# Starting branch A's output projection one or three units earlier in branch B's attention loop

## The chip, the cores and the metric

The kernel runs on one core of a Trainium2 chip. The metric is the device time of one execution in microseconds (us); smaller is better. Engine names are those of the profile: PE (matmul), PEld (weight load), DVE, ACT, POOL, and SP, which here only issues DMAs.

## The reference

One encoder layer, float32, applied to two inputs with the same weights: a prompt of 1024 tokens and a sample of 512 tokens, width 1024.

```python
xn = RMSNorm(x)
z  = xn @ W_in            # q_A k_A v_A q_B k_B v_B gate_A gate_B
o_A = grouped-query attention, q/k normalised per head, rotary positions
o_B = neighbourhood attention on the 64-wide token grid, 8 heads of 64, bias per head
mix = (sigmoid(gate_A) * (o_A @ W_pA) + sigmoid(gate_B) * (o_B @ W_pB)) @ W_out
x = x + mix
x = x + relu(RMSNorm(x) @ W_up)^2 @ W_down
y = RMSNorm(x)
```

The change touches the place where `o_A @ W_pA` is prepared while branch B's attention still runs.

## The kernel before, in words

The two inputs are two passes ("trunks") through the same code, one after the other. The sample goes first: it is the **short** trunk (T = 512, one block of 512 tokens, `first` is true, `JN == 2`). The prompt is the **long** trunk (T = 1024, two blocks, `JN == 1`).

Every matmul is done three times to keep float32 precision: a helper (`split`, lines 189 to 198) cuts a raw float32 tile into a high part, a copy on ACT (line 192), and a low part, two subtractions on DVE (line 198). `mm3` (lines 203 to 205) multiplies high by high, high by low and low by high.

A weight or a row block passes through three steps. SP issues a DMA into a raw tile, ACT and DVE split it into a slot, and PE uses the slot. The raw tiles come from one pool, `rawp`, with **three** buffers, and each tile holds its buffer from the issue of its DMA until DVE has read it for the low part. Weights (`load_cols`, DMA at line 228) and the rows of a branch's attention result (`load_o`, DMA at line 856) share these three buffers.

Branch B's attention runs in units, one head and one group of query blocks at a time: 16 units in the short trunk (two groups for each of 8 heads) and 32 in the long one (four). For each unit, `s_unit` makes the scores (`sbs` on PE, line 1007; maximum and exponent on DVE and ACT, lines 1009 and 1013, result `pbs`), `t_unit` of the unit before transposes them (`ptbs` on PE, split into `bhs` at lines 1041 and 1042), and `v_unit` of the unit before that multiplies by the values (`obs` on PE, line 1064). The values of a head come as 16 small DMAs (`vss`, line 914).

Between these steps PE is fed with **filler**: a generator that yields a few matmuls at a time. In the loop, the filler is first the gate of branch A and B (`gpss`, read out by ACT into `sgs` at line 463, stored by a DMA on ACT's queue as `zgs`), and from unit n-4 (short) or n-8 (long) on it is branch A's projection (`ppas`, with rows `oXs` and weights `w_pas`; the result goes to `mAs` at line 891). Every fourth (short) or eighth (long) unit the next head pair's queries and keys are made (`pqbs`, `pkbs` on PE; `qBs`, `kBs` on ACT and DVE, lines 949 to 969) from weights `w_bqs` and `w_bks`.

`proj_a` is a generator. Its first step, run by `next(pa)`, loads and splits its first weights (`raw_pas_0`, `w_pas_0`) and loads the four row blocks (`rawos_0_0` to `rawos_0_3`, 128 x 512 in the short trunk, 128 x 1024 in the long one) and splits the first three. The split of the fourth is put in the list `held`, which the loop empties one entry per unit. The line that calls `next(pa)` is the one changed.

Engines run their instructions strictly in the order of their streams. That order isn't the order of the code alone: a list scheduler takes the ready operation with the best priority, which is program order, and it hands out pool buffers at the moment it places an operation. So an operation that the code emits earlier can overtake others on every engine, and a buffer goes to whoever is placed first.

Of the kernel before, what the change touches and what calls it, by code (L numbers as in the profile page):

```python
# [61 lines left out]
def encoder(ctx: ExitStack, tc: tile.TileContext, xs, outs, w):  # L62
# [367 lines left out]
    def run(tr, nxt, first):  # L430
# [439 lines left out]
        def proj_a(pool, hold):  # L870
            nxt_w = load_cols(w["w_proj_a"][0], 0, P, f"pa{N}_0", slot_left)
            oA = load_o(0, hold)
            yield
            for c in range(NC8):
                wp = nxt_w
                if c + 1 < NC8:
                    nxt_w = load_cols(w["w_proj_a"][0], (c + 1) * P, P, f"pa{N}_{c + 1}", slot_left)
                else:
                    wp_b.append(load_cols(w["w_proj_b"][0], 0, P, f"pb{N}_0"))
                for tb in range(NB):  # L880
                    if c % 4 == 0:
                        mA[tb, c // 4] = slot([P, 4, 512], F32, f"mA{N}_{tb}_{c}", True)
                    p_ = mm(f"ppa{N}_{c}_{tb}")
                    cs = slice(tb * 512, tb * 512 + 512)
                    za = pool.tile([P, 512], F32, tag="za", name=f"za{N}_{c}_{tb}", bufs=2)
                    nc.sync.dma_start(za, zg[0][c * P : (c + 1) * P, cs])
                    for k in range(4):
                        mm3(p_, wp[k][0], wp[k][1], oA[k][:, 0, cs], oA[k][:, 1, cs], k == 0, k == 3)
                        if k < 3:
                            yield  # L890
                    nc.vector.scalar_tensor_tensor(
                        mA[tb, c // 4][:, c % 4, :], za, 1.0, p_, op0=ALU.add, op1=ALU.mult
                    )
                    yield
# [6 lines left out]
        with phase(f"phB{N}") as ph:  # L901
# [4 lines left out]
            def prep(h):  # L906
                rc = ph.tile([P, 16, 48], F32, tag="rect", name=f"rect{N}_{h}", bufs=2)
                nc.sync.dma_start(rc, biases[:, :, h].rearrange("r c i j -> (r c) i j"))
                rects[h] = rc
                v = slot([P, 4, rows // 4, P], F32R, f"vs{N}_{h}")  # L910
                for j in range(4):
                    c0 = (0, 8, 24, 32)[j]
                    for a in range(4):
                        nc.sync.dma_start(
                            v[a * 32 : a * 32 + 32, j, :, :].bitcast(F32),
                            vd[:, h, :].rearrange("(k a c) d -> a c k d", a=4, c=GRID_W)[a, c0 : c0 + 32],
                        )
                strips[h] = v

            def load_qk(pr, hold=None):  # L920
                return (
                    load_cols(win, 768 + pr * P, P, f"bq{N}_{pr}", hold=hold),
                    load_cols(win, 1280 + pr * P, P, f"bk{N}_{pr}", hold=hold),
                )
# [95 lines left out]
            def t_unit(u):  # L1020
                h, js = u
                nm = f"{N}_{h}_{js[0]}"
                p = PT[u]
                if halves == 2:
                    hl = ph.tile([P, 4, 2, 2, P], F32R, tag="bh", name=f"bh{nm}", bufs=2)
                    todo = [(hf, mm(f"ptb{nm}_{hf}")[:, : nkc * P], slice(hf, hf + nkc), hf) for hf in range(2)]
                else:
                    hl = ph.tile([P, 4, 2, 1, P], F32R, tag="bh", name=f"bh{nm}", bufs=2)
                    pt = mm(f"ptb{nm}")
                    todo = [(0, pt, slice(0, 4), 0)]  # L1030
                    for x in range(4):
                        nc.tensor.transpose(
                            pt[:, x * P : (x + 1) * P], p[:, x // 2, x % 2 * P : (x % 2 + 1) * P], ident
                        )
                for x, pt, ks, hf in todo:
                    if halves == 2:
                        for i in range(nkc):
                            nc.tensor.transpose(pt[:, i * P : (i + 1) * P], p[:, x, i * P : (i + 1) * P], ident)
                    src = pt.rearrange("p (k q) -> p k q", q=P)
                    dh, dl = hl[:, ks, 0, hf, :], hl[:, ks, 1, hf, :]  # L1040
                    nc.scalar.activation(dh, src, AF.Copy)
                    nc.vector.tensor_tensor(dl, src, dh.bitcast(F32), op=ALU.subtract)
                PT[u] = hl
# [63 lines left out]
            n = len(units)  # L1107
# [4 lines left out]
            for i in range(n + LS + LV):  # L1112
                if NB == 1:
                    f = 9 if i < 1 else 5 if i < n - 4 else 6 if i < n else 4 if i == n else 2
                else:
                    f = 0 if i == n - 10 else 5 + (i % 3 > 0) if i < n - 8 else 7
                if i < n:
                    s_unit(units[i])
                    if units[i][1][0] == 1 and units[i][0] + 1 < 8:
                        prep(units[i][0] + 1)  # L1120
                    if i % per == (6 if JN == 1 else 2) and i + 2 < n:
                        while held:
                            held.pop(0)()
                        qp = qkproj(i // per + 1, wqk, qk)
                        for _ in range(NC8):
                            next(qp)
                    if i % per == per - 1 and qp is not None:
                        for _ in qp:
                            pass
                        qp = None  # L1130
                fill.pull(f // 2)
                if 0 <= i - LS < n:
                    t_unit(units[i - LS])
                if held:
                    held.pop(0)()
                if i % per == 0 and i // per < 3:
                    wqk = load_qk(i // per + 1, held)
                if i == n - (6 if first else 9):
                    pa = proj_a(ph, held)
                    next(pa)  # L1140
                if i == n - (4 if JN == 2 else 8):
                    fill.drain()
                    fill.add(pa)
                if qp is not None and NB == 2:
                    for _ in range(NC8):
                        next(qp)
                fill.pull(f - f // 2)
                if 0 <= i - LS - LV < n:
                    v_unit(units[i - LS - LV])
# [730 lines left out]
    for i, tr in enumerate(trunks):  # L1880
        run(tr, trunks[i + 1] if i + 1 < len(trunks) else None, i == 0)
# [66 lines left out]
```

## Time and profile before

| | us |
|---|---|
| time, median of 3 runs | 2131.84 (2130.74 to 2132.03) |
| profiled execution, its own time | 2131.02 |
| its span, first to last instruction | 2129.2 |
| PE busy | 2111.4 (99%) |
| DVE busy | 1471.0 (69%) |
| ACT busy | 1117.3 (52%) |
| POOL busy | 390.7 (18%) |

A busy time is the union of an engine's instructions. PE is busy for nearly the whole span, so the time follows from PE's work plus the few stretches in which PE stands idle. The places of the trace in which the changed step stands lie at 250 to 285 us (short trunk) and at 965 to 1005 us (long trunk).

### The profile page before, as it was taken

How to read it: one execution, taken by the hardware profiler on the slowest of the kernel's cores; microseconds unless marked ns; L12 is line 12 of the kernel's file. 1: busy time of each engine (PE TensorE's matmuls, PEld its weight loads, DVE VectorE, ACT ScalarE, POOL GpSimd, SP SyncE). 2: the span in 40 equal slices, each digit the busy share in tenths (PEclk: the TensorE clock that was granted, in tenths of full speed). 3: DMA queues.
4: the chain of work that ended last, by engine and by line, in shares of the span. 5: the costliest groups of instructions: out<-in, count | busy, mean ns of one | idle time of the engine just before them, and what ended most of it. 6: DMA issues, size and time to landing. Idle time of an engine off the chain costs nothing.

```text
span 2129.2 us, 31802 instructions
## 1 busy us (share of the span) xinstructions
PE 2111.4 (99%) x10967; PEld 1847.8 (87%) x10967; DVE 1471.0 (69%) x2810; ACT 1117.3 (52%) x2351; POOL 390.7 (18%) x508
## 2 busy tenths in 40 slices
PE   9999999999999999999999999999999999999998
PEld 8887788988898888888888999999999988888887
DVE  6674686777667754656782977778777777769563
ACT  5664564566537644655431566566555643434352
POOL 3332420433233323433300200003000000000000
PEclk9999999999999999999999999999999999999999
DMA  6445567521221132433472666578444799688561
GB/s 188 136 125 146 156 192 243 189 72 34 59 85 55 40 110 84 124 105 109 142 247 101 212 197 200 155 247 210 159 146 158 260 353 343 214 279 281 168 197 70
DMA packets 319595, 350.92 MB, mean 165 GB/s; under 512 B 31168, under 2 KB 255048, under 8 KB 319433
## 3 DMA queue, kind: packets, MB, share of 16 engines
q1 hardware_dynamic: 277495, 278.86, 41.7%
q10 hardware_dynamic: 36258, 52.98, 7.1%
q0 software_dynamic: 5680, 17.04, 2.9%
q8 instruction: 87, 1.43, 0.3%
q14 instruction: 75, 0.61, 0.1%
HBM read 264.85 MB, written 87.88 MB: 166 GB/s over the span
## 4 chain that ended last, share of the span: by engine, by line
PE 82%; DVE 2%; DMA 1%; issue 1%; ACT 1%; POOL 1%; SPq 0%; ACTq 0%; POOLq 0%; DVEq 0%
PE dn L205 7%; PE dn L203 7%; PE dn L204 7%; PE pTs L827 3%; PE gpss L203 3%; PE gpss L205 3%; PE gpss L204 3%; PE ud L205 2%; PE uc L205 2%; PE ud L204 2%; PE uc L204 2%; PE uc L203 2%; PE ud L203 2%; PE ua L205 2%; PE ua L204 2%; PE ua L203 2%
## 5 line engine op out<-in xcount | busy, mean ns | idle before, releaser
L205 PE MATMUL dn<-wd,al 128*128 128x512 f32 (+1 forms) x624 | 242.6, 389 | 0.0
L204 PE MATMUL dn<-wd,ah 128*128 128x512 f32 (+1 forms) x624 | 242.6, 389 | 0.0
L203 PE MATMUL dn<-wd,ah 128*128 128x512 f32 (+1 forms) x624 | 242.6, 389 | 0.0
L1361 ACT ACTIVATE ah<-ar 128x512 fp32r<-128x512 f32 x168 | 104.7, 628 | 205.8 <-PE dn L204 181.7
L1362 DVE TENSOR_TENSOR al<-ar,ah 128x512 fp32r<-128x512 f32 x168 | 115.4, 692 | 77.8 <-ACT ah L1361 69.4
L204 PEld LDWEIGHTS dn<-wd,ah 128*128 128x128 f32 x624 | 117.2, 188 | 24.3
L205 PEld LDWEIGHTS dn<-wd,al 128*128 128x128 f32 x624 | 117.2, 188 | 24.1
L203 PEld LDWEIGHTS dn<-wd,ah 128*128 128x128 f32 x624 | 117.2, 188 | 24.0
L793 POOL TENSOR_SCALAR ps<-ps,rls 128x1024 f32<-128x1024 f32 (+1 forms) x96 | 96.8, 1010 | 215.6 <-DVE rls L792 205.0
L833 DVE TENSOR_TENSOR ptls<-pTs,pths 128x512 fp32r<-128x512 f32 x160 | 107.7, 686 | 39.3 <-ACT pths L832 38.8
L832 ACT ACTIVATE pths<-pTs 128x512 fp32r<-128x512 f32 x160 | 94.2, 598 | 74.0 <-PE pTs L827 72.1
L787 DVE TENSOR_REDUCE nms<-ss 128x1 f32<-128x1024 f32 (+1 forms) x96 | 99.6, 1039 | 22.2 <-PE ss L785 21.9
L188 POOL TENSOR_TENSOR rs_f<-ms_f,mhalf 128x1 f32<-128x1 f32 x6 | 4.0, 667 | 590.7 <-DVE ms_f L184 590.7
L203 PE MATMUL gpss<-xs_0h,w_gs 128*128 128x512 f32 x256 | 104.9, 410 | 1.5 <-DVE ptls L833 1.3
L790 ACT ACTIVATE ps<-ss,nms 128x1024 f32<-128x1024 f32 (+1 forms) x96 | 93.2, 972 | 23.1 <-DVE nms L787 20.3
L827 PEld LDWEIGHTS pTs<-ident,ps 128*128 128x128 f32 x640 | 78.2, 140 | 28.0 <-POOL ps L793 4.2
L204 PE MATMUL gpss<-xs_0l,w_gs 128*128 128x512 f32 x256 | 101.1, 395 | 0.0
L205 PE MATMUL gpss<-xs_0h,w_gs 128*128 128x512 f32 x256 | 101.0, 395 | 0.0
L827 PE MATMUL pTs<-ident,ps 128*128 128x128 f32 x640 | 98.9, 274 | 1.2 <-DVE ptls L833 0.3
L1361 ACT ACTIVATE A<-S 128x512 fp32r<-128x512 f32 x128 | 76.1, 624 | 30.5 <-DVE S L1424 26.2
L1362 DVE TENSOR_TENSOR A<-S,A 128x512 fp32r<-128x512 f32 x128 | 84.5, 685 | 3.9 <-ACT A L1361 3.9
L1480 ACT ACTIVATE c<-c 128x384 f32<-128x384 f32 x97 | 50.7, 524 | 68.7 <-DVE c L1479 68.6
(352 smaller groups left out, 6403.6 us busy)
## 6 DMA issues: line engine op xcount, KB each, us to landing
ar<-ud SPq DMA_DIRECT2D x120, 512.0 KB
br<-in_w_mlp_down_dram SPq DMA_DIRECT2D x72, 512.0 KB
rawu<-in_w_mlp_up_dram SPq DMA_DIRECT2D x64, 512.0 KB
ud<-c ACTq DMA_DIRECT2D x128, 192.0 KB
raw_gs<-in_w_in_dram SPq DMA_DIRECT2D x32, 512.0 KB
zgs<-sgs ACTq DMA_DIRECT2D x48, 256.0 KB
ud<-cs SPq DMA_DIRECT2D x64, 192.0 KB
raw_os<-in_w_out_dram SPq DMA_DIRECT2D x16, 512.0 KB
```

What stands on the lines that cost most here:

```text
L203: nc.tensor.matmul(out, ah, bh, start=start, stop=False, **kw)
L204: nc.tensor.matmul(out, ah, bl, start=False, stop=False, **kw)
L205: nc.tensor.matmul(out, al, bh, start=False, stop=stop, **kw)
L787: nc.vector.tensor_reduce(nm_, s, axis=AX.X, op=ALU.max, negate=True)
L790: nc.scalar.activation(p, s, AF.Exp, bias=nm_, accum_out=l)
L793: nc.gpsimd.tensor_scalar(p, p, rl, 1.0, op0=ALU.mult, op1=ALU.mult)
L827: nc.tensor.transpose(pt[:, j * P : (j + 1) * P], PP[u, j][:, kc * P : (kc + 1) * P], ident)
L832: nc.scalar.activation(hi, pt, AF.Copy)
L833: nc.vector.tensor_tensor(lo, pt, hi.bitcast(F32), op=ALU.subtract)
L1361: nc.scalar.activation(hi, src, AF.Copy)
L1362: nc.vector.tensor_tensor(lo, src, hi.bitcast(F32), op=ALU.subtract)
L1480: nc.scalar.activation(t, t, AF.Relu)
```

## The change

One line of the unit loop (line 1138). `n` is 16 in the short trunk and 32 in the long one.

```diff
                 if i % per == 0 and i // per < 3:
                     wqk = load_qk(i // per + 1, held)
-                if i == n - (6 if first else 9):
+                if i == n - (7 if first else 12):
                     pa = proj_a(ph, held)
                     next(pa)
                 if i == n - (4 if JN == 2 else 8):
                     fill.drain()
                     fill.add(pa)
```

Branch A's first step is emitted one unit earlier in the short trunk (unit 9 instead of 10) and three units earlier in the long one (unit 20 instead of 23). No instruction is added or removed; the point at which the projection becomes the filler stays. What moves is the order of the streams. The number after a name's first figures is only a serial number; `0` in `rawos_0_2` stands for branch A and `2` for the row block.

**Short trunk, ACT**, around the splits of the gate's last weights (`w_gs_3328_7`), of the last key weights (`w_bks_3`) and of the projection's first weights and rows. Before:

```order
L1013 ACTIVATE pbs_5_1_3139,ssbs_5_1_3141<-sbss_5_1_0_3147,msbs_5_1_3140 128x256
L192 ACTIVATE w_gs_3328_7_3059<-raw_gs_3328_7_0_3057 128x1024
L1086 DMA obds_102<-os_Bs_3_0_3134 64x2x128
L1013 ACTIVATE pbs_5_1_3139,ssbs_5_1_3141<-sbss_5_2_0_3154,msbs_5_1_3140 128x256
L192 ACTIVATE w_bks_3_3047<-raw_bks_3_0_3045 128x1024
L192 ACTIVATE w_pas_0_3228<-raw_pas_0_0_3226 128x512
L463 ACTIVATE sgs_3328_6_0_3215<-gpss_3328_6_0_3060 128x512
L1041 ACTIVATE bhs_4_0_3218<-ptbs_4_0_3219 128x4x128
```

and now, from the same place (the first `pbs_5_1`) to the split of `w_bks_3`, in two pieces:

```order
L1086 DMA obds_102<-os_Bs_3_0_3161 64x2x128
L192 ACTIVATE w_pas_0_3117<-raw_pas_0_0_3115 128x512
L1013 ACTIVATE pbs_5_1_3166,ssbs_5_1_3168<-sbss_5_2_0_3181,msbs_5_1_3167 128x256
L192 ACTIVATE oXs_0_0_3123<-rawos_0_0_3121 128x512
L463 ACTIVATE sgs_3328_6_0_3245<-gpss_3328_6_0_3060 128x512
```

```order
L1013 ACTIVATE pbs_5_0_3278,ssbs_5_0_3280<-sbss_5_3_0_3295,msbs_5_0_3279 128x256
L192 ACTIVATE oXs_0_1_3129<-rawos_0_1_3127 128x512
L192 ACTIVATE oXs_0_2_3135<-rawos_0_2_3133 128x512
L192 ACTIVATE w_gs_3328_7_3059<-raw_gs_3328_7_0_3057 128x1024
L192 ACTIVATE w_bks_3_3047<-raw_bks_3_0_3045 128x1024
L192 ACTIVATE oXs_0_3_3141<-rawos_0_3_3139 128x512
```

The splits of `w_gs_3328_7` and `w_bks_3` stood ahead of `w_pas_0`; now they stand behind the splits of three row blocks.

**Short trunk, SP**, the DMAs at the same place. Before:

```order
L228 DMA raw_gs_3328_7_0_3057<-in_w_in_dram 128x8x128
L228 DMA raw_pas_0_0_3226<-in_w_proj_a_dram 128x4x128
L908 DMA rects_7_3401<-biases 128x768
L914 DMA vss_6_3161<-vds_98 32x2x128 x16
L856 DMA rawos_0_0_3232<-oads_101 128x512
L856 DMA rawos_0_1_3238<-oads_101 128x512
```

and now:

```order
L228 DMA raw_gs_3328_7_0_3057<-in_w_in_dram 128x8x128
L228 DMA raw_pas_0_0_3115<-in_w_proj_a_dram 128x4x128
L908 DMA rects_7_3401<-biases 128x768
L856 DMA rawos_0_0_3121<-oads_101 128x512
L856 DMA rawos_0_1_3127<-oads_101 128x512
L856 DMA rawos_0_2_3133<-oads_101 128x512
L914 DMA vss_6_3188<-vds_98 32x2x128 x2
L856 DMA rawos_0_3_3139<-oads_101 128x512
L914 DMA vss_6_3188<-vds_98 32x2x128 x14
```

The row blocks moved ahead of the 16 DMAs of `vss_6`. The compiled programs' buffer addresses show one thing more: before, `rawos_0_0` to `rawos_0_2` have three different raw buffers; now `raw_pas_0` and all four `rawos_0` have one and the same, because `raw_gs_3328_7` and `raw_bks_3` hold the other two until their own splits.

**Long trunk, ACT**, around the splits of the row blocks. Before:

```order
L192 ACTIVATE w_pas_0_11204<-raw_pas_0_0_11202 128x512
L967 ACTIVATE kBs_3_0_10995<-pkbs_3_0_11045 64x512 x2
L1069 ACTIVATE ot_Bs_5_1_11075<-obs_5_1_11070 64x512
L1013 ACTIVATE pbs_5_3_11082,ssbs_5_3_11084<-sbss_5_3_1_11099,msbs_5_3_11083 128x384
L1086 DMA obds_4413<-os_Bs_5_1_11077 64x256
L967 ACTIVATE kBs_3_1_10996<-pkbs_3_0_11045 64x512 x2
L192 ACTIVATE oXs_0_0_11210<-rawos_0_0_11208 128x1024
L192 ACTIVATE oXs_0_1_11216<-rawos_0_1_11214 128x1024
```

and now:

```order
L192 ACTIVATE w_pas_0_10891<-raw_pas_0_0_10889 128x512
L192 ACTIVATE oXs_0_2_10909<-rawos_0_2_10907 128x1024
L192 ACTIVATE oXs_0_3_10915<-rawos_0_3_10913 128x1024
L949 ACTIVATE qBs_3_11024<-pqbs_3_0_11027 64x4x128
L1069 ACTIVATE ot_Bs_5_1_11105<-obs_5_1_11100 64x512
L967 ACTIVATE kBs_3_0_11025<-pkbs_3_0_11075 64x512 x2
L463 ACTIVATE sgs_3328_7_1_11235<-gpss_3328_7_1_10961 128x512
L192 ACTIVATE w_pas_1_11306<-raw_pas_1_0_11304 128x512
```

The first two row blocks are now split well before this place (behind `sgs_3328_6_1` and `bhs_5_1`), the last two stand ahead of `qBs_3`, which stood ahead of `w_pas_0` before, and `sgs_3328_7_1` stands here and no longer behind all of `qBs_3` and `kBs_3`. On PE the last nine matmuls of `gpss_3328_7_1`, most of which ran behind `pkbs_3_1`, now run ahead of `pqbs_3_1`; on SP `raw_pas_1` to `raw_pas_4` of the long trunk now go out ahead of the 16 DMAs of `vss_7`.

## The prediction

> **What bounds the kernel now.** I read the page's busy times first, then the waits of PE, then PE's busy time by window around the moved step, and last the instructions of each queue there.
>
> ```profile
> PE 2111.4 (99%) x10967; PEld 1847.8 (87%) x10967; DVE 1471.0 (69%) x2810; ACT 1117.3 (52%) x2351; POOL 390.7 (18%) x508
> ```
>
> PE is the bound: 2111.4 us busy in a span of 2129.2. The change removes no matmul, so it can only fill or open gaps on PE. The gaps near the moved step are few (waits of PE at 240 to 310 us, then at 940 to 1060 us; the columns are total, times, longest):
>
> ```profile
> PE ppas L203 <- ACT sgs L463: 0.7, 1, 0.7
> PE sbs L1007 <- DVE msbs L1009: 0.7, 2, 0.4
> ```
>
> ```profile
> PE obs L1064 <- DVE bhs L1042: 0.7, 2, 0.4
> PE ppas L203 <- ACT w_pas L192: 0.3, 1, 0.3
> PE ppas L203 <- DVE kBs L969: 0.2, 1, 0.2
> ```
>
> The windows (length, then busy us of PE, PEld, DVE, ACT, POOL, then the granted clock) give the same by stage:
>
> ```profile
> 240.00:260.00 20.00, 19.61 (x101) 15.82 (x100) 13.92 (x35) 14.38 (x29) 7.98 (x13) 1.00 0.54 162
> 260.00:275.00 15.00, 15.00 (x74) 12.28 (x74) 9.41 (x28) 8.39 (x17) 4.79 (x6) 1.00 0.56 164
> 275.00:285.00 10.00, 8.90 (x50) 7.21 (x49) 9.12 (x25) 6.20 (x14) 4.08 (x7) 1.00 0.27 79
> 960.00:990.00 30.00, 30.00 (x143) 25.00 (x142) 17.55 (x50) 15.53 (x31) 10.03 (x14) 1.00 0.26 81
> 990.00:1010.00 20.00, 19.09 (x98) 15.11 (x97) 16.87 (x41) 13.51 (x30) 8.27 (x12) 1.00 0.53 159
> ```
>
> PE's idle time in all five is 0.39 + 0 + 1.10 + 0 + 0.91 = 2.4 us. That is the most that the change can gain here, 0.11%. What it can lose isn't capped: PE is fully fed at 260 to 275 and 960 to 990, exactly where the order was moved.
>
> **Short trunk: the row blocks now stand ahead of the gate's weights.** SP before:
>
> ```profile
> 251.52 0.41 SPq L228 DMA_DIRECT2D raw_gs<-in_w_in_dram  x1
> 252.04 0.52 SPq L228 DMA_DIRECT2D raw_pas<-in_w_proj_a_dram  x1
> 252.65 0.46 SPq L908 DMA_DIRECT2D rects<-biases  x1
> 253.20 12.03 SPq L914 DMA_DIRECT2D vss<-vds  x16
> 265.34 4.71 SPq L856 DMA_DIRECT2D rawos<-oads  x4
> ```
>
> The row blocks went out from 265.34, behind 16 small DMAs that held SP for 12 us. On ACT and DVE:
>
> ```profile
> 257.33 1.06 ACT L192 ACTIVATE w_gs<-raw_gs 128x1024 fp32r<-128x1024 f32 x1 [0.71 <-DMA raw_gs<-in_w_in_dram]
> 259.73 0.61 ACT L192 ACTIVATE w_pas<-raw_pas 128x512 fp32r<-128x512 f32 x1
> 268.01 0.63 ACT L192 ACTIVATE oXs<-rawos 128x512 fp32r<-128x512 f32 x1 [0.86 <-DMA rawos<-oads]
> ```
>
> ```profile
> 268.67 1.65 DVE L198 TENSOR_TENSOR oXs<-rawos,oXs 128x256 fp32r<-128x256 f32 x4 [1.04 <-ACT oXs L192]
> ```
>
> Before, `w_gs` of the last gate column was split at 257.33, the moment its data came; PE wanted it more than 5 us later:
>
> ```profile
> 262.55 0.60 PE L1032 MATMUL ptbs<-ident,pbs 128*128 128x128 f32 x4
> 262.91 0.48 PE L203 MATMUL gpss<-xs_0h,w_gs 128*128 128x512 f32 x1
> 265.55 0.40 PE L1007 MATMUL sbs<-kBs,qBs 128*128 128x256 f32 x2
> 265.78 0.40 PE L203 MATMUL pkbs<-xs_0h,w_bks 128*128 128x512 f32 x1
> ```
>
> In the new order that split stands on ACT behind `oXs_0_0`, `oXs_0_1` and `oXs_0_2`. These have one raw buffer between them, shared with `raw_pas_0` too, since the other two buffers belong to the very weights that now wait. So each row block's DMA must wait until DVE has read the block before it: three round trips in series, with `w_gs` behind the third. One trip:
> - from the first row block's issue at 265.34 to its use on ACT at 268.01, 2.67 us;
> - from there to DVE's start at 268.67, 0.66;
> - two subtractions, half of the 1.65 for four, 0.82;
> - from DVE's end to SP's next issue: the fourth block was such a case before. The group of four ended at 265.34 + 4.71 = 270.05 and an issue takes about 0.4 (raw_gs, 0.41), so it went out near 269.65 to 269.7; DVE had finished its first pair at 268.67 + 0.82 = 269.49. I take 0.24.
>
> Together 4.39 us. The start: `raw_pas_0` goes out 0.52 behind `raw_gs`, which was there at 257.33; it is half as large, so I take 258.0 for its split on ACT, now free of `w_gs`. ACT 0.61, DVE 0.82 and the hand-over give the first row block's issue at 259.7. The second goes out at 264.1, the third at 268.5. The third is split from 271.2 to 271.8, and `w_gs` (1.06) is ready at 272.9.
>
> PE gets there much sooner. It had the first `gpss` of that weight at 262.91; four score matmuls are moved ahead of it, which cost 0.46 (a pair keeps PE for 265.78 - 265.55 = 0.23). So PE stands from 263.4 to 272.9: **+9.5 us**. The matmuls queued behind the wait are the rest of this gate column, `obs_4_1` and all of `pkbs_3`; none can overtake on PE. `w_bks_3` follows `w_gs` on ACT with another 1.05 or so while PE works on nine `gpss`, so it adds nothing. Bounds: if landing took 2.0 instead of 2.67, three trips give 7.5. If each took the 5.8 us that the larger `raw_gs` needed (251.52 to 257.33), 19; the row blocks meet less traffic than that one, which had the `vss` DMAs behind it, so I stay near 2.67.
>
> What this frees is the wait at the start of the projection (0.7, `ppas` on `sgs`). On ACT before:
>
> ```profile
> 275.53 1.20 ACT L967 ACTIVATE kBs<-pkbs 64x512 fp32r<-64x512 f32 x2 [0.63 <-DVE kBs L969]
> 276.63 0.62 ACT L192 ACTIVATE oXs<-rawos 128x512 fp32r<-128x512 f32 x1
> 277.27 0.60 ACT L463 ACTIVATE sgs<-gpss 128x512 f32<-128x512 f32 x1
> ```
>
> The fourth row block's split, 0.62 long, stood right ahead of `sgs`; it is behind `w_bks_3` now, well before. **-0.7**, rounded up by what `qBs` and `kBs` gain likewise. The 0.4 and 0.3 on `msbs` I count at nothing: DVE's order there hardly changes. `vss_6`, `raw_pas_1` and the stores go out later, but PE itself is 9 us later; I count them at nothing, with up to +1 if `raw_pas_1` lands behind the first `ppas`.
>
> **Long trunk: 3 units earlier.** Two row blocks are split early, in ACT's slack. The last two stand ahead of `qBs_3`. On PE and ACT before:
>
> ```profile
> 977.81 0.52 PE L1007 MATMUL sbs<-kBs,qBs 128*128 128x384 f32 x2
> 978.16 0.40 PE L203 MATMUL pqbs<-xs_1h,w_bqs 128*128 128x512 f32 x1
> 978.40 0.39 PE L204 MATMUL pqbs<-xs_1l,w_bqs 128*128 128x512 f32 x1
> ```
>
> ```profile
> 977.32 1.19 ACT L967 ACTIVATE kBs<-pkbs 64x512 fp32r<-64x512 f32 x2 [2.31 <-PE pkbs L205]
> 982.37 2.00 ACT L192 ACTIVATE oXs<-rawos 128x1024 fp32r<-128x1024 f32 x2
> 993.53 0.60 ACT L463 ACTIVATE sgs<-gpss 128x512 f32<-128x512 f32 x1
> ```
>
> The slots of the last two blocks come free with the last `pkbs` of the block, so ACT starts them at 977.3, not sooner. Then two `oXs` (2.00), `qBs` and `ot_Bs` (about 0.6 each, as `sgs`), two `kBs` (1.19) and `sgs` (0.60) end at 982.3. PE reaches `pqbs_3_1` at 978.16 plus nine moved `gpss` at 0.24 (the distance of the two `pqbs`), 980.3, and there it now waits for the PSUM bank that `sgs` reads out: about 2.0 by the sum of durations, 1.6 if ACT's instructions overlap slightly. I take **+1.9**, near the former. Against it, `raw_pas_1` goes out ahead of the `vss` DMAs, which removes the 0.3 on `w_pas`: **-0.3**. Net +1.6, bounds -1.2 (all of the 0.7, 0.3 and 0.2 gone and no new wait) and +3.
>
> **A slow restart of PE.** A 9.5 us gap is longer than any that this trace shows in its middle. The nearest row is the kernel's start, after idleness:
>
> ```profile
> 7.64 1.94 PE L410 MATMUL ptxs<-ident,xns 128*128 128x128 f32 x8 [1.03 <-DVE xns L152]
> 10.72 0.41 PE L203 MATMUL zs<-wghs,xs_0h 128*128 128x256 f32 x1
> 10.93 0.42 PE L204 MATMUL zs<-wgls,xs_0h 128*128 128x256 f32 x1
> 12.85 0.35 PE L204 MATMUL zs<-wgls,xs_0h 128*128 128x256 f32 x1
> 13.28 0.28 PE L204 MATMUL zs<-wgls,xs_0h 128*128 128x256 f32 x1
> 13.40 0.28 PE L205 MATMUL zs<-wghs,xs_0l 128*128 128x256 f32 x1
> ```
>
> Until 12.85 the same matmul comes every 0.21 us, from 13.28 every 0.12, with the same clock written in the profile. So a PE coming from idleness runs at a little over half speed for some microseconds: 12.85 - 7.64 = 5.2 at most, and a dense stretch of about 3.6. It would lose about half of that: 0 if 9.5 us of idleness aren't enough, 2.6 at most. I take 1.8, half the dense stretch, since a gap of 9.5 us lies nearer to that start than to the gaps of 0.7 after which nothing shows. The Trainium skill, page "TensorE: Matmul & The Clock Gate", Part 1, has it that one idle window of about 3.4 us puts PE's clock back to half until a busy window has passed; the trace's start agrees in kind, and its middle, without any such gap, can't say. By that rule the sum is 2143.2, without it 2141.4.
>
> **Sum.** 9.5 - 0.7 + 1.6 + 1.8 = +12.2 on the profiled execution's 2131.0, so 2143.2. The median of the runs is 0.8 above the profiled one; I leave that inside the range.
>
> **Rivals.**
> - *The stall, but no slow restart.* For it: the granted clock reads 1.00 in every window, the first ones too, so the profile shows no throttle at all. 2141.4; with a slightly faster landing, 2139.
> - *A part of the stall.* If the third trip isn't ahead of `w_gs` in time (say the third block's DMA meets a free buffer), one trip of 4.4 goes, and the restart with it: about 2137. Against it: one address for all four blocks.
> - *The change only feeds PE sooner (not slower).* The `w_gs` split would have to be done by 263.4; that holds only if the three trips took less than 1.3 us each, from 258.7 to 262.3 with 1.06 for `w_gs` itself. Then the gaps of 2.4 go, 2128.6, which is still within 0.2% of before. Against it: DVE's and ACT's share of a trip alone is 1.5.
> - *It does nothing that can be measured.* The long trunk's +1.6 and the short one's relief cancel, with no stall: about 2131 to 2133. It needs the same as the rival before.
>
> **How the numbers follow.** Chances: stall with slow restart 0.50, stall without 0.33, a part of it 0.06, nothing 0.08, gaps closed 0.03. The first two span 7.5 to 11 for the stall, -1.2 to +3 for the long trunk and 0 to 2.6 for the restart; taken together, not all at one end, 2136.5 to 2147. 0.2% of the time, 4.3 us, is about what a measurement of this kernel tells from no change; slower by more means over 2136.1, which takes the first two cases and two thirds of the third: 0.87. Within it 0.11, faster 0.02, the rest of the two last cases and of the third.
>
> **What the changed profile would show.** PE idle for 7 to 11 us near 263, put down to ACT's `w_gs` split at line 192. Three `rawos` issues on SP about 4.4 us apart, each just behind a DVE split. `gpss` matmuls right behind the gap at about 0.42 apart instead of 0.24 if the slow restart is real. No 0.7 wait of `ppas` on `sgs`. In the long trunk, a wait of `pqbs` on `sgs` of 1 to 2 us near 980. I am wrong if `w_gs` is split before 264, or if the three issues follow each other at once.

## The result and the profile after

The change makes the kernel slower: 2146.57 us (2144.21 to 2147.04, 6 runs) against 2131.90 (6 runs of before), a ratio of 1.0065 (1.0055 to 1.0074) on record; the two medians differ by +14.7 us, a ratio of 1.0069. The forecast was 2143.2 in a range of 2136.5 to 2147.0. The profiled execution of the change took 2144.21, 13.2 more than that of before; it is the fastest of the six, and the account of the prediction below says what probably sets it apart.

PE does the same number of matmuls (busy us of each engine):

```profile
PE 2114.0 (99%) x10967; PEld 1848.1 (86%) x10967; DVE 1470.3 (69%) x2810; ACT 1117.2 (52%) x2351; POOL 389.2 (18%) x508
```

The span grew by 13.2 us and PE's busy time by 2.6. So some 10.6 us are idle time, and 2.6 are matmuls that took longer or no longer overlap; the slow matmuls shown below make 1.5 of these. The waits of PE, at 240 to 320 us and then at 940 to 1070:

```profile
PE gpss L203 <- ACT w_gs L192: 8.0, 1, 8.0
PE sbs L1007 <- DVE msbs L1009: 1.7, 5, 0.6
```

```profile
PE pqbs L203 <- ACT sgs L463: 1.7, 1, 1.7
PE sbs L1007 <- DVE kBs L969: 0.8, 1, 0.8
PE sbs L1007 <- DVE msbs L1009: 0.5, 1, 0.5
PE obs L1064 <- DVE bhs L1042: 0.3, 1, 0.3
```

One wait of 8.0 us for the split of `w_gs` dominates. The old 0.7 of `ppas` on `sgs` is gone, but the waits of the scores on their maximum rose from 0.7 to 1.7; 0.62 of that rise lies just ahead of the 8.0. In the long trunk there is the expected wait of `pqbs`, and another, on `kBs`, that the prediction did not have. The same by window, with the granted clock after the five busy times:

```profile
260.00:275.00 15.00, 6.42 (x26) 4.96 (x26) 6.49 (x17) 6.07 (x11) 2.44 (x5) 0.80 0.33 98
275.00:285.00 10.00, 10.00 (x47) 8.29 (x47) 4.71 (x14) 4.77 (x9) 0.73 (x1) 0.96 0.49 135
285.00:310.00 25.00, 24.22 (x130) 19.53 (x129) 20.55 (x57) 15.81 (x37) 8.39 (x14) 1.00 0.49 143
```

At 260 to 275 PE was busy for all 15 us before, and now for 6.4, and the clock, which read 1.00 there before, reads 0.80.

The cause, instruction by instruction: SP's issues of the row blocks, ACT's splits, and PE (start, duration, then the group).

```profile
259.62 8.81 SPq L856 DMA_DIRECT2D rawos<-oads  x3
268.53 0.85 SPq L914 DMA_DIRECT2D vss<-vds  x2
```

```profile
258.12 0.63 ACT L192 ACTIVATE w_pas<-raw_pas 128x512 fp32r<-128x512 f32 x1 [1.49 <-POOL bms L993]
...
262.16 0.63 ACT L192 ACTIVATE oXs<-rawos 128x512 fp32r<-128x512 f32 x1 [2.91 <-DMA rawos<-oads]
...
266.61 0.63 ACT L192 ACTIVATE oXs<-rawos 128x512 fp32r<-128x512 f32 x1 [0.91 <-DMA rawos<-oads]
270.83 0.63 ACT L192 ACTIVATE oXs<-rawos 128x512 fp32r<-128x512 f32 x1 [3.59 <-DMA rawos<-oads]
271.36 1.04 ACT L192 ACTIVATE w_gs<-raw_gs 128x1024 fp32r<-128x1024 f32 x1
```

```profile
262.89 0.48 PE L1007 MATMUL sbs<-kBs,qBs 128*128 128x256 f32 x2
264.00 0.50 PE L1007 MATMUL sbs<-kBs,qBs 128*128 128x256 f32 x2 [0.62 <-DVE msbs L1009]
272.46 0.80 PE L203 MATMUL gpss<-xs_0h,w_gs 128*128 128x512 f32 x1 [7.95 <-ACT w_gs L192]
273.05 0.63 PE L204 MATMUL gpss<-xs_0l,w_gs 128*128 128x512 f32 x1
...
275.18 0.63 PE L203 MATMUL gpss<-xs_0h,w_gs 128*128 128x512 f32 x1
275.61 0.45 PE L204 MATMUL gpss<-xs_0l,w_gs 128*128 128x512 f32 x1
275.90 0.40 PE L205 MATMUL gpss<-xs_0h,w_gs 128*128 128x512 f32 x1
```

Three splits of row blocks follow each other at distances of 4.45 and 4.22 us, each released by its own DMA, and `w_gs` comes right behind the third. Its DMA had gone out at 251.54; in the kernel before it went out at 251.52, and the data were there at 257.33. Then PE's `gpss` come 0.43 apart until 275.6 (the first two 0.59), and 0.29 and 0.23 apart from there.

Matching the matmuls of the two traces in their order gives PE's delay, here at the times of the kernel before: 0.0 us at 262, 10.3 from 270 to 276, 9.6 at 277, 9.9 at 300, 9.9 at 975, 11.9 at 981, 12.5 at 1020, 12.5 at 1160 and 13.2 from 1190 to the end.

### The profile page after: what moved, and what is told of

It reads as the page before. It is cut to its first block, busy times and chain, and to the rows that moved or that the text cites. A ratio compares the mean times of both kernels' runs of the same rounds, so it can differ in the third digit from the quotient of the medians.

```text
span 2142.4 us, 31806 instructions
## 1 busy us (share of the span) xinstructions
PE 2114.0 (99%) x10967; PEld 1848.1 (86%) x10967; DVE 1470.3 (69%) x2810; ACT 1117.2 (52%) x2351; POOL 389.2 (18%) x508
## 4 chain that ended last, share of the span: by engine, by line
PE 81%; DVE 2%; DMA 2%; issue 1%; ACT 1%; POOL 1%; SPq 0%; ACTq 0%; POOLq 0%; DVEq 0%
PE dn L204 7%; PE dn L205 7%; PE dn L203 7%; PE pTs L827 3%; PE gpss L203 3%; PE gpss L205 3%; PE gpss L204 3%; PE uc L203 2%; PE ud L203 2%; PE ud L205 2%; PE uc L205 2%; PE ud L204 2%; PE uc L204 2%; PE ua L203 2%; PE ua L205 2%; PE ua L204 2%
## 5 line engine op out<-in xcount | busy, mean ns | idle before, releaser
L1013 ACT ACTIVATE pbs<-sbss,msbs 128x384 f32<-128x384 f32 (+1 forms) x96 | 55.5, 578 | 60.6 <-DVE msbs L1009 27.7
```

The lines of the kernel that those rows point to most:

```text
L1013: nc.scalar.activation(p[:, x], sb, AF.Exp, bias=nm_[:, x : x + 1], scale=-1.0, accum_out=l[:, x : x + 1])
```

## Experiments

The experiments ran in three groups, each on one chip and beside its own runs of the kernel before (medians 2133.03, 2132.36 and 2132.44). A difference in us is between medians of one group.

**The short trunk alone, and the long trunk alone.** The one line, with the other trunk's number left as it was:

```diff
-                if i == n - (7 if first else 12):
+                if i == n - (7 if first else 9):     # short trunk alone
+                if i == n - (6 if first else 12):    # long trunk alone
```

> The short trunk's half alone: 7 from the end in the short trunk, 9 in the long one as before. Theory (three round trips through one raw buffer ahead of the split of w_gs, then PE at half clock): PE idle about 8 us near 264, released by the split of w_gs; behind it 8 to 16 matmuls 0.43 apart; in all +10 to +12 us, nearly all of the change's +14.7. Rival (the long trunk's move costs most, and the short one's gap is partly given back later): +5 or less.

Measured: 2142.83, ratio 1.0047 (1.0034 to 1.0061), +9.8 us. That is just under the 10 to 12 expected. The same kernel in a later group, for comparison:

> The short trunk's half once more, for comparison with the one before on the same chip. Both theories: +9.5 to +10.5 over before, clock 0.5 for 7 to 10 us from about 267 on.

2142.73, ratio 1.0048 (1.0036 to 1.0061), +10.3 us. PE's wait for `w_gs` is 7.9 us in both, and the clock is at half for 10.24 us behind it in both.

> The long trunk's half alone: 12 from the end in the long trunk, 6 in the short one as before. Theory: a 1.7 us wait of pqbs on sgs near 981, a small one on kBs near 995, the clock stays at 1.00 throughout, +2 to +3.5 us in all. Rival (moving the long trunk's request is free, all of the loss is the short trunk's): 0 +- 0.5.

Measured: 2135.16, ratio 1.0011 (1.0002 to 1.0019), +2.1 us. Its waits at 940 to 1070 are the same as the change's:

```profile
PE pqbs L203 <- ACT sgs L463: 1.7, 1, 1.7
PE sbs L1007 <- DVE kBs L969: 0.8, 1, 0.8
```

So both halves lose, the short one most. The short half's rival (+5 or less) falls by the time. The long half's (0, give or take 0.5) falls by these rows; its time alone, with an interval of +0.4 to +4.0 us, would not settle it.

**Two round trips in place of three.** The split of the third row block is put off too:

```diff
-                if hold is None or k < 3:
+                if hold is None or k < (2 if first else 3):   # with 7 and 9
```

> Short trunk's request at 7 (long 9), but the split of the third row block is put off too, as the fourth's is already, so that two round trips and no longer three stand ahead of the split of w_gs. Theory (each trip through the shared raw buffer costs 4.4 us): PE idle 8.0 - 4.4 = 3.6 us; too short for the clock to fall in most executions, so the total is +3.5 to +4.5 us and not two thirds of the whole. Rival (the idle is set by something else, such as traffic of the DMA queues): the idle stays at 7 to 8 us.

Measured: 2139.78, ratio 1.0032 (1.0020 to 1.0045), +6.8 us. PE and ACT:

```profile
268.99 0.79 PE L203 MATMUL gpss<-xs_0h,w_gs 128*128 128x512 f32 x1 [4.24 <-ACT w_gs L192]
...
271.07 0.63 PE L203 MATMUL gpss<-xs_0h,w_gs 128*128 128x512 f32 x1
271.50 0.63 PE L204 MATMUL gpss<-xs_0l,w_gs 128*128 128x512 f32 x1
```

```profile
267.36 0.63 ACT L192 ACTIVATE oXs<-rawos 128x512 fp32r<-128x512 f32 x1 [1.41 <-DMA rawos<-oads]
267.89 1.04 ACT L192 ACTIVATE w_gs<-raw_gs 128x1024 fp32r<-128x1024 f32 x1
```

The wait fell from 7.9 to 4.2 us; one trip is worth 3.7. That part of the theory holds. What it said of the clock was wrong: `gpss` are 0.43 apart here too, and with these slow matmuls the total stays above the 3.5 to 4.5 expected. It fell by 3.0 against the short trunk alone; what lies between 3.0 and 3.7 was not taken apart.

**The same order on ACT, two buffers.** All put-off splits are made just before the request. That of `w_bks` is one of them, so its raw buffer is free for the row blocks:

```diff
                 if i == n - (7 if first else 9):
+                    while held:
+                        held.pop(0)()
                     pa = proj_a(ph, held)
```

> Short trunk's request at 7 (long 9), but all put-off splits are made just before it. The last key weights w_bks are then split early and give back their raw buffer, so the row blocks go through two buffers in turn; the split of w_gs still stands behind all three row blocks on ACT. Theory (it is the one shared buffer, not the order on ACT by itself): the first row block is asked for some 6 us sooner, w_gs is split near 264, PE idle 0.5 to 2 us, no slow clock, +0.5 to +2 us. Rival (any split of w_gs behind three row blocks stalls PE): idle still 6 us or more.

Measured: 2135.30, ratio 1.0013 (1.0004 to 1.0021), +2.3 us. Waits at 240 to 320:

```profile
PE sbs L1007 <- DVE msbs L1009: 2.6, 4, 1.6
PE gpss L203 <- ACT w_gs L192: 1.5, 1, 1.5
```

`w_gs` still stands behind three row blocks on ACT, and the wait is 1.5 us instead of 7.9. So it is the one shared buffer that makes the wait long. (SP asks for the first row block at 254.19 here, against 260.23 in the short trunk alone: the second buffer gives both an earlier start and shorter turns, and this run doesn't tell the two apart.) The total is a little over the 2 us expected; one score waits 1.6 us for its maximum.

**No row block ahead of the weights.** The splits of all four row blocks put off (`k < (0 if first else 3)`, with 7 and 9):

> Short trunk's request at 7 (long 9), but the splits of all four row blocks are put off, one per unit. The split of w_gs and of w_bks then stands ahead of the row blocks on ACT and the blocks get three buffers. Theory (the order around the raw buffers is all that the earlier request cost): no idle of PE at 264, clock 1.00, within 1 us of before. Rival (asking sooner costs by itself, through the later vss DMAs or the tile slots): +3 us or more stays.

Measured: 2132.86, ratio 1.0002 (0.9993 to 1.0011). The short trunk's loss is gone, at the same early request (the interval is -1.5 to +2.3 us). Nothing was won either:

```profile
260.00:275.00 15.00, 14.86 (x71) 12.12 (x70) 10.74 (x31) 9.57 (x19) 4.71 (x7) 1.00 0.61 178
275.00:285.00 10.00, 9.64 (x52) 7.66 (x51) 8.60 (x22) 6.54 (x15) 3.89 (x7) 1.00 0.30 86
```

The idle time at 275 to 285 fell from 1.10 to 0.36, and small waits came at other places.

**The request at the end of the loop's body.** The two lines of the request moved behind the second `fill.pull`, in the same unit (7; long 9):

> Short trunk's request in the same unit as in the change, 7 from the end, but at the end of the loop's body instead of its middle (long 9). The split of w_gs is then ahead of the row blocks, that of w_bks behind three of them, with two buffers for the blocks. Theory (the first weight behind the row blocks stalls its matmuls): no idle at gpss, about 2.5 us of idle of pkbs on ACT's split of w_bks, clock 1.00, +1.5 to +2.5 us. Rival (only w_gs is critical): no idle above 1 us, same as before.

Measured: 2133.81, ratio 1.0007 (0.9998 to 1.0016), +1.5 us, not told apart from no change. The wait is there, on the other weight, but at 1.0 us instead of 2.5. That is at the rival's bound of 1 us, so this run settles neither. Two of PE's waits at 240 to 320:

```profile
PE pkbs L203 <- ACT w_bks L192: 1.0, 1, 1.0
PE ptbs L1032 <- POOL pbs L1017: 0.7, 1, 0.7
```

**One unit more in the long trunk** (13 and 6):

> Long trunk's request at 13 (short 6). One unit earlier than the change, a third row block is split early, so that one of them (1.06 us) and w_pas_1 stand behind the last key matmuls on ACT ahead of sgs_7_1, and no longer two. Theory (the wait of pqbs on sgs is ACT's queue behind the slot of the last row blocks): the wait falls from 1.7 to 0.7 us, total about 1 us under that of 12 from the end, so +1 over before. Rival (the earlier, the worse): the wait stays 1.7 or grows, +2 or more.

Measured: 2136.38, ratio 1.0016 (1.0007 to 1.0025), +4.0 us. The wait of `pqbs` is 1.6 us. ACT between the last key matmul and `sgs`:

```profile
979.88 1.06 ACT L192 ACTIVATE oXs<-rawos 128x1024 fp32r<-128x1024 f32 x1 [1.79 <-PE pkbs L205]
980.97 0.59 ACT L1069 ACTIVATE ot_Bs<-obs 64x512 f32<-64x512 f32 x1
981.59 0.59 ACT L949 ACTIVATE qBs<-pqbs 64x512 fp32r<-64x512 f32 x1
982.08 0.60 ACT L1013 ACTIVATE pbs<-sbss,msbs 128x384 f32<-128x384 f32 x1
982.59 0.19 ACT L1013 ACTIVATION_READ_ACCUMULATOR pbs<-sbss,msbs 128x1 f32 x1
982.68 1.18 ACT L967 ACTIVATE kBs<-pkbs 64x512 fp32r<-64x512 f32 x2
983.88 0.60 ACT L463 ACTIVATE sgs<-gpss 128x512 f32<-128x512 f32 x1
```

One row block is gone from the queue, but an exponent (0.79) took its place. So the expectation of 0.7 failed, and the rival's numbers (1.7 or more, +2 or more) came nearer. That ACT's queue ahead of `sgs` makes the wait is seen in the rows; how much of it is the row blocks' was not separated, nor why the total is 1.9 above that of 12 from the end (the two intervals overlap).

**The halves together again.** The change once more, and the change with the short trunk's splits put off:

> The change itself once more, beside the others on one chip. Theory (the two trunks' losses add up): 9.8 + 2.1 = +12 us over before, with 2 us up or down by where the half-clock windows of 3.4 us fall against PE's idle time. Rival (the two halves make each other worse): +14 us or more here too.

Measured: 2146.38, ratio 1.0066 (1.0053 to 1.0078), +14.0 us. That is the upper end of the theory and the lower end of the rival, so it settles neither.

> Both trunks' requests as in the change (7 and 12), with the splits of the short trunk's row blocks put off as in the kernel that put off all four. Theory (the whole of the short trunk's loss is the order around its raw buffers, and the long trunk's loss stands apart from it): +2 to +3 us, that of the long trunk's half alone. Rival (the two halves make each other worse): +4 us or more.

Measured: 2135.20, ratio 1.0015 (1.0006 to 1.0024), +2.8 us: the long trunk's loss without the short one's. That is under the +4 of its rival. 9.8 to 10.3 and 2.1 to 2.8 make 12 to 13 of the 14.0 to 14.7. Some 0.8 of the rest is a wait at 1180 us (`pt` on ACT's line 340), which both profiles of the change show and those of the halves don't. Why it appears stays open, and with it whether the halves simply add up.

**The clock apart from the idle time.** In the short trunk alone (7 and 9), 34 more matmuls fill the wait; the column's first real matmul overwrites what they wrote:

```diff
                     g_ = mm(f"gps{nm}")
+                    for j in range(34 if first and goff == 3328 and c == 7 else 0):
+                        nc.tensor.matmul(g_, xh(tb, 0)[:, :P], xh(tb, j % NC8), start=True, stop=True)
```

> The short trunk's half (7 and 9) with 34 more matmuls of 128x512 ahead of the gate column that waits; their results are overwritten by the column's first real matmul. They take 34 x 0.228 = 7.8 us of the idle time, so that PE isn't idle for a whole window. Theory (after some 8 us of idleness PE runs at half clock for 3 to 5 us): the wait for w_gs ends at the same time, the clock stays 1.00 in all windows, and the total is 1.5 to 2.5 us less than the short trunk's half alone, about +7.5 to +8.5 over before. Rival (the slow matmuls come from late weights, not from the clock): they stay 0.43 apart and the total stays at +9.8.

Measured: 2141.01 (2140.63 to 2144.69), ratio 1.0045 (1.0032 to 1.0057), +8.6 us, 1.7 less than the short trunk alone in the same group; the two intervals overlap, so the 1.7 isn't shown by the times alone. The profiled execution is the slowest of the five, and in it the clock fell after all (windows of 3.41 us):

```profile
272.04:275.45 3.41, 1.56 (x10) 1.19 (x9) 1.65 (x4) 2.49 (x3) 0.00 (x0) 1.00 0.16 55
275.45:278.87 3.42, 3.42 (x11) 2.75 (x11) 2.20 (x4) 1.85 (x4) 0.72 (x1) 0.50 0.47 138
```

PE was idle for only 1.9 us there, in a stretch of 3.41 in which it was busy for 1.56. The expectation that the clock would stay at 1.00 was missed in this execution. It was met in two others, 2141.01 and 2142.50 us: their mean granted clock is 1.000 on record, and a window of 3.41 us at half would take 0.0008 off it. In the short trunk alone all ten executions have 0.997.

This execution also tells a slow clock from late weights, the rival. The matmuls behind the wait begin at full speed, 0.33 and 0.24 apart, and come 0.42 apart from 275.39 on, where the column turns to 0.50 (275.45):

```profile
274.59 0.50 PE L203 MATMUL gpss<-xs_0h,w_gs 128*128 128x512 f32 x1 [1.85 <-ACT w_gs L192]
274.92 0.40 PE L204 MATMUL gpss<-xs_0l,w_gs 128*128 128x512 f32 x1
275.16 0.39 PE L1066 MATMUL obs<-bhs,vss 128*128 128x256 f32 x2
275.39 0.62 PE L205 MATMUL gpss<-xs_0h,w_gs 128*128 128x512 f32 x1
275.81 0.63 PE L203 MATMUL gpss<-xs_0h,w_gs 128*128 128x512 f32 x1
```

## Why the prediction was right

- **Three round trips.** Predicted 4.39 us each, first issue at 259.7, `w_gs` ready at 272.9. Measured 4.45 and 4.22, first issue at 259.62, `w_gs` ready at 272.40 and PE's first matmul at 272.46. PE stood for 8.6 us (0.62 and 7.95), against 9.5. In a trip, the landing took 2.54 to 2.96 us (2.67 was taken) and the hand-over from DVE to SP 0.07 (0.24). The start was right in part by luck: the row puts ACT's wait ahead of the split of `w_pas` (1.49 us, until 258.12) down to POOL, and not to the landing from which 258.0 was worked out. The kernel with two trips and the one with two buffers show the mechanism, and the one with no block ahead shows that it is the short trunk's whole loss.
- **The slow restart.** Predicted 1.8. In the profile there are seven distances of 0.43 (the first 0.59) in place of 0.23, 1.5 us (272.46 to 275.61 is 3.15; seven at 0.23 would be 1.6). The clock column shows half clock for 6.83 us, half of it in the idle time. In the second profile of the change it is 10.24 us, and PE's delay at 300 us is 11.2 instead of 9.9. That is more than half of what lies between the first profile and the median: the rival without a restart is out. (8.6 and 1.5 make 10.1, and the delay behind them is 10.3.)
- **The clock at the kernel's start.** The prediction read 1.00 there beside matmuls at half speed, and its rival took that for a profile without throttle. The column isn't a reading there: the trace's clock record begins at 13.00 us in the kernel before, and the matmuls go from 0.21 to 0.11 us apart at 13.05. In the kernel with 34 more matmuls the record begins at 16.04, and the same step comes at 16.09.
- **The window.** The Trainium skill, page "TensorE: Matmul & The Clock Gate", Part 1, has a free-running window of 3413 ns by which the clock is set. The stretches at half clock here, 3.41, 6.83 and 10.24 us, are one, two and three such windows; the trace agrees. That a whole idle window is needed, as the same part of the Trainium skill has it, isn't borne out: the windows after which the clock fell had PE busy for 0.00, 0.26, 0.51, 0.52, 1.45 and 1.56 us of 3.41.
- **The relief of 0.7.** It came as predicted: PE's delay falls from 10.3 to 9.6 us where the projection starts. But some 0.3 of it was lost again up to 300 us (9.9), where scores wait for DVE's maximum longer than before. The step "DVE's order there hardly changes" was wrong, by that much.
- **The long trunk.** Predicted +1.9 for the wait and -0.3. The wait is 1.72, PE's delay rises by 2.0 there. The -0.3 was mis-sized: the wait on `w_pas` is gone, but 0.8 on `kBs` came, and the trunk costs 2.6 in the profile in place of 1.6. DVE splits `kBs` as soon as before, 1.66 us behind the start of the last `pkbs` matmul (1.65 before). PE gets to the scores that need it sooner: eight `gpss` stood between the last `pkbs` and these scores before, and they now run ahead of `pqbs`.
- **Outside.** 0.8 at 1180, which I had no term for.

The sum of the profiled execution, 13.2, stands against 12.2, and it is that near in part by luck. The stall with its restart was taken 1.0 too large (11.3 against 10.3), and the other terms 2.0 too small (+0.9 against +2.9). The median is 14.7 above before, 0.4 us inside the range. The other five executions have a mean granted clock of 0.997 instead of 0.998, as one more window at half clock would give, though only the second profile shows it directly.

Two slips in the working changed nothing. The range of 2136.5 to 2147 is the sum of all low and of all high ends, though it is called "not all at one end". And the rival that only feeds PE sooner counts its trips from 258.7, while the first issue was put at 259.7; that leaves it 0.9 us for a trip, and not 1.3.

## What to carry to other kernels

When a request is moved ahead, ask whose buffer it takes: in a pool of three, two raw tiles whose readers now stood behind the request left one buffer for four loads, and a rotation became a chain of round trips. Follow each engine's queue to the first instruction that another engine waits for, and price it by round trips times their number. And where the matmul engine will stand idle for some microseconds, add the slow matmuls behind the gap.

## What the runs showed of the hardware

The clock falls sooner than I had thought: a gap of 1.9 us was enough where it fell into one window, with PE busy for 46% of it. A gap of 1.7 us in one window, with PE busy for 50%, left the clock at 1.00, in the change, in the long trunk alone, and in the change with the short trunk's splits put off. This window is of the long trunk alone:

```profile
981.07:984.48 3.41, 1.69 (x8) 1.14 (x7) 2.92 (x11) 3.05 (x6) 1.06 (x2) 1.00 0.60 175
```

So in these traces the step lies between 46% and 50% of a window's busy time as the profile counts it. The clock comes back after a window that is busy nearly throughout (3.26 of 3.41 us in the first profile of the change); one with 2.02 us of 3.41 did not bring it back:

```profile
264.54:267.95 3.41, 0.26 (x2) 0.05 (x1) 1.42 (x7) 1.57 (x5) 2.03 (x4) 1.00 0.53 156
267.95:271.37 3.42, 0.00 (x0) 0.00 (x0) 0.41 (x2) 0.24 (x1) 0.00 (x0) 0.50 0.33 96
271.37:274.78 3.41, 2.02 (x5) 1.59 (x6) 2.80 (x6) 2.28 (x3) 0.00 (x0) 0.50 0.28 88
274.78:278.19 3.41, 3.41 (x12) 2.83 (x11) 2.10 (x7) 1.44 (x3) 0.00 (x0) 0.50 0.26 74
```

These are the four windows of the change's second profile. Where the window's edges lie against the gap differs from execution to execution, so nearly the same idle time costs 1.5 us of slow matmuls in the first profile, and in the second, with a delay 1.3 us larger, nearly 3.
